# A hybrid decoder layer in split float32: who issues which transfer, and how many places the weights have

## The chip, the cores and the metric

The kernel runs on one core of a Trainium2 chip. The metric is device time of one execution in microseconds (us), as the median of three runs. The engines of the core are TensorE (PE, matmuls; PEld are its weight loads), VectorE (DVE), ScalarE (ACT), GpSimd (POOL) and SyncE (SP, here an issuer of DMA transfers and nothing else). Every engine works through its own list of instructions in order and waits at the first one whose inputs or places are not ready. DMA transfers are issued by such an instruction too, on SyncE, ScalarE or GpSimd.

## The reference

One layer for 2048 new prompt tokens and for 8 x 8 sample tokens with a past, width 1024. Norms stand around both halves, the mixer has four retention heads and four gated-delta heads of 128, and the MLP has 4096 channels:

```python
h = _rmsnorm(x, pre_mix_w)
m, S_r, S_g, new_conv = _hybrid_mixer(h, ...)   # w_in: 1024 -> 4104
x = x + _rmsnorm(m, post_mix_w)                 # w_out is inside the mixer
h = _rmsnorm(x, pre_mlp_w)
f = jnp.square(jax.nn.relu(jnp.einsum('bld,df->blf', h, w_up)))
f = jnp.einsum('blf,fd->bld', f, w_down)
x = x + _rmsnorm(f, post_mlp_w)
```

```python
# a gated-delta head, for each chunk of positions
A = jnp.where(strict, bi[..., :, None] * kk * dmat, 0.0)
sol = lax.linalg.triangular_solve(eye + A, rhs, left_side=True, lower=True, unit_diagonal=True)
v_new = u - jnp.einsum('bhcd,bhde->bhce', w, S)
```

Retention keeps a decayed state per head; the delta heads have a short convolution ahead of them and solve a unit lower triangular system in each chunk. Outputs are the new rows and all states.

## The kernel before

**Products.** All is float32. A matmul operand is split into a high part and the rest, hi and lo, and each product is three matmuls (hi by hi, hi by lo, lo by hi). The prompt is worked in four blocks of T = 512 tokens; the second block also carries the 64 sample tokens. A block runs: statistics of its rows (`stats`, L485), its normed and split transpose (`prep`, L505), the input projection with the heads (`proj`, L1192), the output projection (`out_proj`, L1225), the second norm (`norm2`, L1269), the MLP (`mlp`, L1385) and the last norm with the residual (`finish_half`, L1396). The projections of a block are merged with the MLP of the block before it, so TensorE takes a few matmuls of the one and then of the other.

**Weights** (`load_unit`, L342). A unit is mostly four pieces. The first block loads a raw piece (L359, tag `wraw`), ScalarE writes its hi part (L360), and VectorE or GpSimd its lo part (L361, two pieces of four each), both into a 512 KB place with the tag `wpc`; the pair is stored in DRAM (L363, `ws`). Later blocks load the pair back (L365). There are WB = 6 places `wpc` and RB = 5 places `wraw`. The places `wraw` also take the rows and transposed features that `stats` and `prep` load (L490, L523), the mixer rows that come back from DRAM (`load_mix`, L568), and in the last block the residual rows `x1d` (L1423); in the other blocks those go through the two places `raw`.

**The delta heads' inverse** (`gdn_head`, L785 to L845). VectorE inverts small diagonal blocks; the data are turned between partitions by 19 small transfers a head in three stages: L797, L798 and L804; L823, L824 and L826; L839. After each stage VectorE waits for them. TensorE later transposes the result `XX` (L271). There are 16 heads over the four blocks.

**The MLP's square** (`up`, L1312): ScalarE writes relu into `raw` and its square, rounded to the hi part, into `fhi`; GpSimd squares `raw` exactly in place (L1325); VectorE takes the difference into `flo`.

**What sets the order.** TensorE's order is the order in which the program writes its instructions (L267, L271). A planner (`Weave`, L122) decides it when the program is built: it merges the generators of heads, projections and MLP by due times, which come from a table of latencies (L100). The other engines are ordered by the framework's scheduler, which lays out a timeline of its own (L1519) and so may put any instruction of SyncE, ScalarE, VectorE or GpSimd earlier or later than it is written. In the kernel before nearly all transfers are issued by SyncE.

Of the kernel before, what the change touches and what calls it, by code (L numbers as in the profile page):

```python
# [202 lines left out]
def hybrid_kernel(ctx: ExitStack, tc: tile.TileContext, I, O, NB: int, SB: int):  # L203
    nc = tc.nc
    PS = bass.MemoryType.PSUM
    NTM = T + NS
    WB = 6
    RB = 5
    HP = 100
# [132 lines left out]
    def load_unit(name, idx, n, ncol):  # L342

        src = I[name]
        for i in idx:
            src = src[i]
        per = 2 if ncol <= NU else 1
        w = per * ncol
        first = (name, idx) not in stored
        if first:  # L350
            stored[name, idx] = [wst.tile([P, 2 * w], F32, tag=nm("ws"), name=nm("ws")) for q in range(n // per)]
        his, los = [], []
        for q in range(n // per):
            fit = lambda t: t.rearrange("p (a c) -> p a c", a=per)
            both = page([P, 4 * NU], "wpc", F32R, bufs=WB)
            hi, lo = fit(both[:, :w]), fit(both[:, w:2 * w])
            if first:
                r = fit(page([P, 2 * NU], "wraw", bufs=RB)[:, :w])
                nc.sync.dma_start(r, src[:, per * q:per * (q + 1), :])  # L359
                act(hi, r, AF.Copy)  # L360
                tt(lo, r, hi.bitcast(F32), ALU.subtract, eng=(V, G)[TUNE["pool"][q % 4]])  # L361
                if NB > 1:
                    nc.sync.dma_start(stored[name, idx][q], both[:, :2 * w].bitcast(F32))  # L363
            else:
                nc.sync.dma_start(both[:, :2 * w].bitcast(F32), stored[name, idx][q])  # L365
            his.append(hi)
            los.append(lo)
        return (lambda k: his[k // per][:, k % per, :]), (lambda k: los[k // per][:, k % per, :])
# [43 lines left out]
    class Block:  # L412
# [72 lines left out]
        def stats(self):  # L485
            samp = self.samp
            ssh, ssq = small([P, 2, 8], "ssh", bufs=1), small([P, 8], "ssq", bufs=1)
            for t, (c0, rows) in enumerate(self.tiles):
                for hf in range(2):
                    xv = page([P, 2 * NU], "wraw", bufs=RB)[:rows, :T]  # L490
                    nc.sync.dma_start(xv, self.x_rows(t)[:, hf * T:(hf + 1) * T])
                    act(xv, xv, AF.Square, accum_out=ssh[:rows, hf, t:t + 1])
                    yield self.lat["st"]
# [11 lines left out]
        def prep(self):  # L505
            b, samp, NT, rstd = self.b, self.samp, self.NT, self.rstd
            yield self.lat["rstd"]
            hhi, hlo = self.place()
            dg = page([P, 2 * NU], "wraw", bufs=RB)[:, :T]
            tt(v4(dg), bc4(ident), per4(rstd[:, :NC]), ALU.mult)  # L510
# [11 lines left out]
            for k in range(KT):  # L522
                xk = page([P, 2 * NU], "wraw", bufs=RB)[:, :T]  # L523
                nc.sync.dma_start(xk, I["xpT"][b, k])
                parts = [(xk, 0, T, rB[0])]
                if samp:
                    xq = small([P, NS], "xq")
                    nc.sync.dma_start(xq, I["xsT"][k])
                    parts.append((xq, T, NT, rB[1]))
# [31 lines left out]
        def load_mix(self):  # L561
            self.mix = self.place()
            for e in self.order:
                for part in range(2 if self.samp else 1):
                    yield self.key(("e", "s")[part] + str(e))
                    if (e, part) in self.away:
                        c0, n = ((0, T), (T, NS))[part]
                        st = page([P, 2 * NU], "wraw", bufs=RB)[:, :n]  # L568
                        nc.sync.dma_start(st, self.mixd[e, :, c0:c0 + n])
                        self.split_mix(e, st, c0, n)  # L570
                W.signal(self.key(f"m{e}"), self.lat["mem"])
# [150 lines left out]
        def gdn_head(self, h):  # L722
# [73 lines left out]
            for c in range(NC):  # L796
                nc.sync.dma_start(prod[NB16 * c:NB16 * (c + 1), :BB * BB], cm2[:, c, :])  # L797
            nc.sync.dma_start(m2, prod[:nb, :BB * BB].unsqueeze(1).to_broadcast([nb, P // nb, BB * BB]))  # L798
            xtf = XT.rearrange("p c d -> p (c d)")[:nb]
# [3 lines left out]
            for c in range(NC):  # L803
                nc.sync.dma_start(w32[NB16 * c:NB16 * (c + 1)].rearrange("b j i -> b (j i)"), cm[:, c, :])  # L804
            two = lambda ap: ap.rearrange("p (u x) -> p u x", u=2)[:, :, :HB * BB].rearrange("p u (c r) -> p u c r", c=HB)
# [16 lines left out]
            blocks = xf[:nb, :BB * BB]  # L822
            nc.sync.dma_start(x1, blocks.rearrange("p (g x) -> p g x", g=g))  # L823
            nc.sync.dma_start(x2, xf[1:nb:2, :BB * BB].unsqueeze(1).to_broadcast([nb // 2, 2 * g, BB * BB]))  # L824
            for c in range(NC):
                nc.sync.dma_start(xc[:, c, :], blocks[NB16 * c:NB16 * (c + 1)])  # L826
            x1, z, ro = (ap.rearrange("p (r i) -> p r i", r=g) for ap in (x1, z, ro))
# [10 lines left out]
            for c in range(NC):  # L838
                nc.sync.dma_start(cm[:, c, :], ro[g * NB16 * c:g * NB16 * (c + 1)].rearrange("p r i -> p (r i)"))  # L839
            blk = lambda ap: ap.rearrange("p (b i) -> p b i", b=NB16).unsqueeze(1).to_broadcast([P, NC, NB16, BB])  # L840
# [68 lines left out]
        def gdn_sample(self, h):  # L909
# [4 lines left out]
            Ss = page([P, NSEQ, P], "Ss")  # L914
            nc.sync.dma_start(Ss, I["state_gdn"][h])
            pk = mx()
# [155 lines left out]
        def proj_ret(self, h):  # L1072
            samp, b = self.samp, self.b
            get, vd, gt, vds = self.vg[h]
            rt = get(1).rearrange("p (a i) -> p a i", a=2)
            nc.sync.dma_start(rt, I["rope"][:, :, b * T:(b + 1) * T])
            wu = load_unit("w_ret", (h, 0), KT, UNIT)
            qk = get(2).rearrange("p (a i) -> p a i", a=2)
            qks = rts = None
            if samp:  # L1080
                qks, rts = small([P, 2, NS], "qks", bufs=1), small([P, 2, NS], "rts", bufs=1)
                nc.sync.dma_start(rts, I["rope"][:, :, NB * T:])
            for a in range(2):
# [53 lines left out]
        def ret_sample(self, h):  # L1137
# [4 lines left out]
            Ss = page([P, NSEQ, P], "Ss")  # L1142
            nc.sync.dma_start(Ss, I["state_ret"][h])
            pt = mx()
# [80 lines left out]
        def out_proj(self, then=None):  # L1225
# [5 lines left out]
            for n, src in enumerate(("post_mix_w", "pre_mlp_w")):  # L1231
                w = page([P, D_MODEL], "kq", bufs=2) if self.b else page([P, D_MODEL], atag[n])
                nc.sync.dma_start(w, I[src].to_broadcast([P, D_MODEL]))
                wB.append(w)
# [34 lines left out]
        def norm2(self, t, m, sq, wB):  # L1269
# [9 lines left out]
            for hf in range(2):  # L1279
                x = page([P, NTM], "raw", bufs=2)[:rows, :T]  # L1280
                nc.sync.dma_start(x, self.x_rows(t)[:, hf * T:(hf + 1) * T])
                mh = mr[:, hf * T:(hf + 1) * T]
# [29 lines left out]
        def up(self, f, wu, ft, mi, n0, n1):  # L1312
# [10 lines left out]
            for hi, lo, v in parts:  # L1323
                act(hi, v, AF.Square)
            tt(r[:, :w], r[:, :w], r[:, :w], ALU.mult, eng=G)  # L1325
            for hi, lo, v in parts:
# [69 lines left out]
        def finish_half(self, t, u):  # L1396
# [7 lines left out]
            if u == 0 and t == 0:  # L1404
                self.r3 = small([P, 5, 2], "r3", bufs=1)
                self.w3 = page([P, D_MODEL], "vz")
                nc.sync.dma_start(self.w3, I["post_mlp_w"].to_broadcast([P, D_MODEL]))
            r = self.r3[:, t]
# [13 lines left out]
            for cols in half:  # L1422
                x = (page([P, 2 * NU], "wraw", bufs=RB) if tail else page([P, NTM], "raw", bufs=2))[:rows, :T]  # L1423
                nc.sync.dma_start(x, self.x1d[c0:c0 + rows, cols])
                stt(av[:, cols], av[:, cols], r[:rows, 0:1], x, ALU.mult, ALU.add)
# [106 lines left out]
```

## Time and profile before

| What | Value |
|---|---|
| Median of three runs | 3095.73 us (3091.30 to 3099.69) |
| Profiled execution | 3096.51 us |
| Its span, first to last instruction | 3094.7 us |
| TensorE busy | 2864.7 us, 93% |
| VectorE, ScalarE, GpSimd busy | 1552.2, 793.0, 603.0 us |
| Mean granted TensorE clock | 0.978 |
| Transfers on the hardware queue q1 | 229008 packets, 559.07 MB, 53.6% of 16 engines |
| Transfers on the software queue q0 | 7760 packets, 26.56 MB, 2.2% |

The span is the time from the first to the last instruction of the profiled execution. An engine that is busy for a small share can still be waited for, so the table says where to look and not what to gain. The granted clock is a share of TensorE's full speed, 2.4 GHz. Busy times of GpSimd are rough. Weights and the split copies make most of the traffic: 612 loads `wpc<-ws` of 512 KB and 204 stores `ws<-wpc`, all issued by SyncE.

### The profile page before, as it was taken

Reading aid. Unit: us, or ns where it says so; the run is one execution under the profiler, and the core shown is the slowest. Engines: PE = TensorE matmul, PEld = TensorE weight load, DVE = VectorE, ACT = ScalarE, POOL = GpSimd, SP = SyncE. Lnnn points to the kernel's source line nnn. Section 1 sums busy time; section 2 is a strip of 40 time slices with the busy share of each in tenths; the row PEclk is TensorE's granted clock in tenths of the full one; section 3 lists DMA queues with packets and bytes.
Section 4 is the critical chain, followed back from the end, with each engine's and each line's share of the span. In section 5 each row is a group of like instructions: output and inputs, shape, how many; then the busy total and the mean of one; then the engine's idle time right before and its main releaser. Section 6 shows DMA issues by size and latency. Waiting matters only on the chain.

```text
span 3094.7 us, 43223 instructions
## 1 busy us (share of the span) xinstructions
PE 2864.7 (93%) x16072; PEld 2456.4 (79%) x16072; DVE 1552.2 (50%) x3386; ACT 793.0 (26%) x2199; POOL 603.0 (19%) x610
## 2 busy tenths in 40 slices
PE   7888889999999898999999999899999999899998
PEld 6677788878888687888887888777878787787776
DVE  6978667474756526552535252456353544331112
ACT  4343423233323323322212222221112221210111
POOL 4232113231233313111101111211110111120101
PEclk9999999999999999999999999999999999999999
DMA  8645655666565666645444444565554554665554
GB/s 296 224 161 170 219 206 197 206 210 209 166 217 208 215 220 241 235 144 174 145 157 149 154 158 157 184 218 176 178 172 165 167 186 158 225 233 190 186 186 168
DMA packets 238130, 590.49 MB, mean 191 GB/s; under 512 B 63072, under 2 KB 71648, under 8 KB 237920
## 3 DMA queue, kind: packets, MB, share of 16 engines
q1 hardware_dynamic: 229008, 559.07, 53.6%
q0 software_dynamic: 7760, 26.56, 2.2%
q8 instruction: 127, 2.08, 0.3%
q10 hardware_dynamic: 1152, 2.10, 0.2%
q14 instruction: 83, 0.68, 0.1%
HBM read 443.02 MB, written 137.79 MB: 188 GB/s over the span
## 4 chain that ended last, share of the span: by engine, by line
PE 65%; DMA 14%; DVE 13%; issue 2%; SPq 2%; ACT 2%; POOL 1%; DVEq 0%; POOLq 0%; ACTq 0%
PE mm L267 57%; DMA wpc<-ws 8%; PE mx L267 7%; PE mx L271 2%; DVE ym L255 1%; DVE XX L255 1%; DVE mt L255 1%; DVE raw L255 1%; ACT junk L249 1%; DVE wpc L255 1%; DMA wraw<-in_x_prompt 1%; DVE XX L252 1%; DMA raw<-in_x_prompt 1%; DMA ym<-xf 1%; DMA ym<-ym 1%
## 5 line engine op out<-in xcount | busy, mean ns | idle before, releaser
L267 PE MATMUL mm<-ahi,wpc 128*128 128x512 f32 (+2 forms) x3040 | 880.3, 364 | 38.1 <-DMA wpc<-ws 32.6
L267 PE MATMUL mm<-wpc,fhi 128*128 128x512 f32 x2048 | 665.5, 406 | 47.9 <-DMA wpc<-ws 31.9
L267 PEld LDWEIGHTS mm<-ahi,wpc 128*128 128x128 f32 x3040 | 547.8, 191 | 127.9 <-DMA wpc<-ws 39.6
L267 PE MATMUL mm<-alo,wpc 128*128 128x512 f32 (+2 forms) x1520 | 540.4, 355 | 1.4 <-DVE alo L255 1.4
L267 PEld LDWEIGHTS mm<-wpc,fhi 128*128 128x128 f32 x2048 | 381.2, 192 | 150.7 <-DMA wpc<-ws 45.2
L267 PE MATMUL mm<-bhi,wpc 128*128 128x512 f32 (+2 forms) x1536 | 428.0, 353 | 11.9 <-DMA wpc<-ws 9.4
L267 PE MATMUL mm<-wpc,flo 128*128 128x512 f32 x1024 | 410.3, 401 | 8.0 <-DVE flo L255 8.0
L267 PE MATMUL mm<-wpc,bhi 128*128 128x256 f32 (+1 forms) x1664 | 301.2, 286 | 23.5 <-DMA wpc<-ws 22.2
L267 PEld LDWEIGHTS mm<-alo,wpc 128*128 128x128 f32 x1520 | 290.6, 191 | 34.4 <-DVE alo L255 1.6
L249 ACT ACTIVATE raw<-mm 128x512 f32<-128x512 f32 (+2 forms) x226 | 114.8, 509 | 786.9 <-PE mm L267 741.1
L267 PEld LDWEIGHTS mm<-bhi,wpc 128*128 128x128 f32 x1536 | 274.6, 190 | 46.2 <-DMA wpc<-ws 11.6
L255 POOL TENSOR_TENSOR raw<-raw 128x512 f32<-128x512 f32 (+2 forms) x166 | 151.1, 911 | 821.3 <-ACT fhi L249 670.2
L255 DVE TENSOR_TENSOR a<-a,mm 128x512 f32<-128x512 f32 x224 | 152.3, 684 | 255.9 <-PE mm L267 255.6
L267 PEld LDWEIGHTS mm<-wpc,bhi 128*128 128x128 f32 x1664 | 253.2, 190 | 28.2 <-DMA wpc<-ws 25.9
L267 PE MATMUL mm<-blo,wpc 128*128 128x512 f32 (+2 forms) x768 | 265.3, 345 | 0.0
L255 DVE TENSOR_TENSOR flo<-raw,fhi 128x512 fp32r<-128x512 f32 (+1 forms) x166 | 103.1, 622 | 307.7 <-POOL raw L255 307.7
L267 PEld LDWEIGHTS mm<-wpc,flo 128*128 128x128 f32 x1024 | 196.2, 192 | 56.3 <-DVE flo L255 10.8
L267 PE MATMUL mm<-wpc,blo 128*128 128x256 f32 (+1 forms) x768 | 216.4, 282 | 0.2 <-DVE blo L255 0.2
L255 POOL TENSOR_TENSOR wpc<-wraw,wpc 128x512 fp32r<-128x512 f32 (+1 forms) x104 | 145.7, 1413 | 338.4 <-ACT wpc L249 280.8
L249 ACT ACTIVATE wpc<-wraw 128x512 fp32r<-128x512 f32 (+1 forms) x208 | 129.4, 629 | 233.0 <-PE mm L267 151.6
L267 PEld LDWEIGHTS mm<-blo,wpc 128*128 128x128 f32 x768 | 146.3, 191 | 14.5
L267 PEld LDWEIGHTS mm<-wpc,blo 128*128 128x128 f32 x768 | 146.3, 190 | 0.4 <-DVE blo L255 0.4
(486 smaller groups left out, 3611.7 us busy)
## 6 DMA issues: line engine op xcount, KB each, us to landing
wpc<-ws SPq DMA_DIRECT2D x612, 512.0 KB
ws<-wpc SPq DMA_DIRECT2D x204, 512.0 KB
wraw<-in_w_up SPq DMA_DIRECT2D x64, 256.0 KB
wraw<-in_w_down SPq DMA_DIRECT2D x64, 256.0 KB
raw<-in_x_prompt SPq DMA_DIRECT2D x32, 256.0 KB
wraw<-in_w_ret SPq DMA_DIRECT2D x28, 256.0 KB
wpc<-ws SPq DMA_DIRECT2D x12, 528.0 KB
mixd<-raw POOLq DMA_DIRECT2D x24, 256.0 KB, 4.7
```

The source lines that it names most:

```text
L249: return A.activation(out, in_, f, **kw)
L252: return V.scalar_tensor_tensor(out=out, in0=in0, scalar=scalar, in1=in1, op0=op0, op1=op1)
L255: return (eng or V).tensor_tensor(out=out, in0=a, in1=b, op=op)
L267: return tc.keep_in_program_order(nc.tensor.matmul(out, lhsT, rhs, start=start, stop=stop))
L271: return tc.keep_in_program_order(nc.tensor.transpose(out, in_, ident[:rows, :rows]))
```

## The change

The places `wpc` become eight, the places `wraw` three, and a new tag `xin` has two places for a 128 x 512 tile. SyncE keeps the raw weights (L359), the split weights (L365) and the last block's `x1d`. GpSimd now issues the stores of split weights, all small transfers of the inverse, the sample states, the rotary tables, the norm weights, the rows `x` of the second norm, the `x1d` of the other blocks, and the mixer rows, which go to `xin`. ScalarE issues the loads of `stats` and `prep`, into `xin` too. The exact square at L1325 goes to ScalarE. The scratch that the framework keeps for GpSimd's transfers is set to 8192 bytes at the end of the program. In counts: GpSimd issues 642 more transfers (208 stores, 304 of the inverse, 130 others), ScalarE 58, and 166 squares change engine. The lines keep their numbers.

```diff
@@ -207,2 +207,2 @@
-    WB = 6
-    RB = 5
+    WB = 8
+    RB = 3
@@ -363 +363 @@
-                    nc.sync.dma_start(stored[name, idx][q], both[:, :2 * w].bitcast(F32))
+                    nc.gpsimd.dma_start(stored[name, idx][q], both[:, :2 * w].bitcast(F32))
@@ -490,2 +490,2 @@
-                    xv = page([P, 2 * NU], "wraw", bufs=RB)[:rows, :T]
-                    nc.sync.dma_start(xv, self.x_rows(t)[:, hf * T:(hf + 1) * T])
+                    xv = page([P, T], "xin", bufs=2)[:rows]
+                    nc.scalar.dma_start(xv, self.x_rows(t)[:, hf * T:(hf + 1) * T])
@@ -509 +509 @@
-            dg = page([P, 2 * NU], "wraw", bufs=RB)[:, :T]
+            dg = page([P, T], "xin", bufs=2)
@@ -523,2 +523,2 @@
-                xk = page([P, 2 * NU], "wraw", bufs=RB)[:, :T]
-                nc.sync.dma_start(xk, I["xpT"][b, k])
+                xk = page([P, T], "xin", bufs=2)
+                nc.scalar.dma_start(xk, I["xpT"][b, k])
@@ -528 +528 @@
-                    nc.sync.dma_start(xq, I["xsT"][k])
+                    nc.scalar.dma_start(xq, I["xsT"][k])
@@ -568,2 +568,2 @@
-                        st = page([P, 2 * NU], "wraw", bufs=RB)[:, :n]
-                        nc.sync.dma_start(st, self.mixd[e, :, c0:c0 + n])
+                        st = page([P, T], "xin", bufs=2)[:, :n]
+                        nc.gpsimd.dma_start(st, self.mixd[e, :, c0:c0 + n])
@@ -797,2 +797,2 @@
-                nc.sync.dma_start(prod[NB16 * c:NB16 * (c + 1), :BB * BB], cm2[:, c, :])
-            nc.sync.dma_start(m2, prod[:nb, :BB * BB].unsqueeze(1).to_broadcast([nb, P // nb, BB * BB]))
+                nc.gpsimd.dma_start(prod[NB16 * c:NB16 * (c + 1), :BB * BB], cm2[:, c, :])
+            nc.gpsimd.dma_start(m2, prod[:nb, :BB * BB].unsqueeze(1).to_broadcast([nb, P // nb, BB * BB]))
@@ -804 +804 @@
-                nc.sync.dma_start(w32[NB16 * c:NB16 * (c + 1)].rearrange("b j i -> b (j i)"), cm[:, c, :])
+                nc.gpsimd.dma_start(w32[NB16 * c:NB16 * (c + 1)].rearrange("b j i -> b (j i)"), cm[:, c, :])
@@ -823,2 +823,2 @@
-            nc.sync.dma_start(x1, blocks.rearrange("p (g x) -> p g x", g=g))
-            nc.sync.dma_start(x2, xf[1:nb:2, :BB * BB].unsqueeze(1).to_broadcast([nb // 2, 2 * g, BB * BB]))
+            nc.gpsimd.dma_start(x1, blocks.rearrange("p (g x) -> p g x", g=g))
+            nc.gpsimd.dma_start(x2, xf[1:nb:2, :BB * BB].unsqueeze(1).to_broadcast([nb // 2, 2 * g, BB * BB]))
@@ -826 +826 @@
-                nc.sync.dma_start(xc[:, c, :], blocks[NB16 * c:NB16 * (c + 1)])
+                nc.gpsimd.dma_start(xc[:, c, :], blocks[NB16 * c:NB16 * (c + 1)])
@@ -839 +839 @@
-                nc.sync.dma_start(cm[:, c, :], ro[g * NB16 * c:g * NB16 * (c + 1)].rearrange("p r i -> p (r i)"))
+                nc.gpsimd.dma_start(cm[:, c, :], ro[g * NB16 * c:g * NB16 * (c + 1)].rearrange("p r i -> p (r i)"))
@@ -915 +915 @@
-            nc.sync.dma_start(Ss, I["state_gdn"][h])
+            nc.gpsimd.dma_start(Ss, I["state_gdn"][h])
@@ -1076 +1076 @@
-            nc.sync.dma_start(rt, I["rope"][:, :, b * T:(b + 1) * T])
+            nc.gpsimd.dma_start(rt, I["rope"][:, :, b * T:(b + 1) * T])
@@ -1082 +1082 @@
-                nc.sync.dma_start(rts, I["rope"][:, :, NB * T:])
+                nc.gpsimd.dma_start(rts, I["rope"][:, :, NB * T:])
@@ -1143 +1143 @@
-            nc.sync.dma_start(Ss, I["state_ret"][h])
+            nc.gpsimd.dma_start(Ss, I["state_ret"][h])
@@ -1233 +1233 @@
-                nc.sync.dma_start(w, I[src].to_broadcast([P, D_MODEL]))
+                nc.gpsimd.dma_start(w, I[src].to_broadcast([P, D_MODEL]))
@@ -1281 +1281 @@
-                nc.sync.dma_start(x, self.x_rows(t)[:, hf * T:(hf + 1) * T])
+                nc.gpsimd.dma_start(x, self.x_rows(t)[:, hf * T:(hf + 1) * T])
@@ -1325 +1325 @@
-            tt(r[:, :w], r[:, :w], r[:, :w], ALU.mult, eng=G)
+            act(r[:, :w], r[:, :w], AF.Square)
@@ -1407 +1407 @@
-                nc.sync.dma_start(self.w3, I["post_mlp_w"].to_broadcast([P, D_MODEL]))
+                nc.gpsimd.dma_start(self.w3, I["post_mlp_w"].to_broadcast([P, D_MODEL]))
@@ -1424 +1424 @@
-                nc.sync.dma_start(x, self.x1d[c0:c0 + rows, cols])
+                (nc.sync if tail else nc.gpsimd).dma_start(x, self.x1d[c0:c0 + rows, cols])
@@ -1528 +1528 @@
-    nc = bacc.Bacc("TRN2", target_bir_lowering=False, num_devices=1)
+    nc = bacc.Bacc("TRN2", target_bir_lowering=False, num_devices=1, dynamic_dma_scratch_size=8192)
```

TensorE's order stays as it was but for the names of three tiles. SyncE's list goes from 1375 rows to 859, GpSimd's from 602 to 886 and ScalarE's from 1760 to 1982.

**First place: SyncE at the end of the second block.** The names `wpc_...<-ws_...` are loads of split weights into their places, the first four of the last unit before the merged stage and then of the next; `raw_...<-x1d_...` are residual rows for the last norm. Before:

```order
L365 DMA wpc_3413_18880<-ws_973_4987 128x1024
L365 DMA wpc_3414_18882<-ws_975_4988 128x1024
L1424 DMA raw_3407_18854<-x1d_4_115 128x512
L1424 DMA raw_3408_18857<-x1d_4_115 128x512
L1424 DMA raw_3418_18901<-x1d_4_115 128x512
L1424 DMA raw_3419_18904<-x1d_4_115 128x512
L365 DMA wpc_3415_18884<-ws_977_4989 128x1024
L365 DMA wpc_3416_18886<-ws_979_4990 128x1024
L365 DMA wpc_3438_19051<-ws_1026_5272 128x1024
L365 DMA wpc_3439_19053<-ws_1028_5273 128x1024
L1424 DMA raw_3424_18937<-x1d_4_115 128x512
L1424 DMA raw_3425_18940<-x1d_4_115 128x512
```

and now:

```order
L365 DMA wpc_3413_18880<-ws_973_4987 128x1024
L365 DMA wpc_3414_18882<-ws_975_4988 128x1024
L365 DMA wpc_3415_18884<-ws_977_4989 128x1024
L365 DMA wpc_3416_18886<-ws_979_4990 128x1024
L365 DMA wpc_3438_19051<-ws_1026_5272 128x1024
L365 DMA wpc_3439_19053<-ws_1028_5273 128x1024
L365 DMA wpc_3440_19055<-ws_1030_5274 128x1024
L365 DMA wpc_3441_19057<-ws_1032_5275 128x1024
```

The residual rows are gone from between the loads of weights, and eight of those follow each other.

**Second place: between the second and the third stage of the inverse, last delta head of the second block.** `ym_...<-xf` (L826) ends the second stage and `ym_...<-ym` (L839) is the third; `ws_...<-wpc_...` are stores of split weights, `wraw_...<-in_w_up` loads of raw ones. On SyncE before:

```order
L826 DMA ym_2006_9928<-xf_82 128x1x16 x4
L363 DMA ws_2099_10340<-wpc_2106_10349 128x1024
L359 DMA wraw_2144_10490<-in_w_up 128x512
L363 DMA ws_2101_10341<-wpc_2108_10355 128x1024
L359 DMA wraw_2146_10496<-in_w_up 128x512
L363 DMA ws_2103_10342<-wpc_2110_10361 128x1024
L359 DMA wraw_2175_10620<-in_w_up 128x512
L363 DMA ws_2132_10473<-wpc_2139_10477 128x1024
L359 DMA wraw_2177_10626<-in_w_up 128x512
L363 DMA ws_2134_10474<-wpc_2141_10483 128x1024
L359 DMA wraw_2179_10632<-in_w_up 128x512
L839 DMA ym_2006_9928<-ym_2006_9928 128x1x16 x4
```

On GpSimd now, with its splits of weights (`TENSOR_TENSOR wpc`) and reloads of mixer rows (`xin_...<-mixd`) in the same list:

```order
L826 DMA ym_2006_9928<-xf_82 128x1x16 x2
L363 DMA ws_2101_10341<-wpc_2108_10355 128x1024
L363 DMA ws_2103_10342<-wpc_2110_10361 128x1024
L363 DMA ws_2097_10339<-wpc_2104_10343 128x1024
L363 DMA ws_2099_10340<-wpc_2106_10349 128x1024
L255 TENSOR_TENSOR wpc_2139_10477<-wraw_2140_10478,wpc_2139_10477 128x512
L569 DMA xin_2001_9901<-mixd_3_114 128x512
L255 TENSOR_TENSOR wpc_2141_10483<-wraw_2142_10484,wpc_2141_10483 128x512
L363 DMA ws_2136_10475<-wpc_2143_10489 128x1024
L363 DMA ws_2138_10476<-wpc_2145_10495 128x1024
L839 DMA ym_2006_9928<-ym_2006_9928 128x1x16 x4
```

The stores have moved to GpSimd with the inverse's transfers and stand between its stages there, now beside GpSimd's own splits; the raw loads stay on SyncE.

## Rows read from the trace of the kernel before

**Rows 1.** The page's busy times: us, share of span, instructions

```profile
PE 2864.7 (93%) x16072; PEld 2456.4 (79%) x16072; DVE 1552.2 (50%) x3386; ACT 793.0 (26%) x2199; POOL 603.0 (19%) x610
```

**Rows 2.** Waits of TensorE: whom for, us in total, times, longest us

```profile
PE mm L267 <- DMA wpc<-ws: 96.2, 89, 5.6
PE mx L271 <- DVE XX L255: 23.6, 5, 10.1
PE mm L267 <- DVE flo L255: 8.0, 5, 3.1
```

**Rows 3.** Timeline of SyncE, end of the second block: start us, us, engine, line, operation

```profile
2006.12 6.34 SPq L1424 DMA_DIRECT2D raw<-x1d  x4
2012.55 2.17 SPq L365 DMA_DIRECT2D wpc<-ws  x4
```

**Rows 4.** Timeline of TensorE, matmuls behind a late reload; idle before in brackets

```profile
395.23 0.38 PE L267 MATMUL mm<-bhi,wpc 128*128 128x256 f32 x1 [2.57 <-DMA wpc<-ws]
...
1929.70 0.50 PE L267 MATMUL mm<-wpc,bhi 128*128 128x256 f32 x2 [2.14 <-DMA wpc<-ws]
...
1943.08 0.50 PE L267 MATMUL mm<-wpc,bhi 128*128 128x256 f32 x2 [1.64 <-DMA wpc<-ws]
...
2019.37 0.58 PE L267 MATMUL mm<-ahi,wpc 128*128 128x256 f32 x1 [4.96 <-DMA wpc<-ws]
...
3029.66 0.73 PE L267 MATMUL mm<-wpc,fhi 128*128 128x512 f32 x2 [0.33 <-DMA wpc<-ws]
```

**Rows 5.** Windows of 10 us: each engine's busy us, PEclk, DMA share, GB/s

```profile
1970.00:1980.00 10.00, 5.56 (x13) 4.40 (x14) 3.04 (x7) 1.44 (x4) 1.64 (x3) 0.68 0.91 363
...
2000.00:2010.00 10.00, 10.00 (x45) 7.38 (x44) 7.29 (x14) 4.77 (x12) 4.96 (x6) 0.96 0.24 88
```

**Rows 6.** Windows of two stages, same columns

```profile
1120.00:1220.00 100.00, 86.57 (x572) 79.37 (x571) 38.44 (x79) 27.48 (x85) 19.65 (x24) 0.91 0.60 205
...
1960.00:2040.00 80.00, 65.27 (x336) 53.34 (x336) 43.34 (x81) 23.34 (x62) 27.73 (x33) 0.89 0.61 213
```

**Rows 7.** Groups of GpSimd and ScalarE: busy us, mean ns

```profile
L255 POOL TENSOR_TENSOR raw<-raw 128x512 f32<-128x512 f32 (+2 forms) x166 | 151.1, 911 | 821.3 <-ACT fhi L249 670.2
...
L255 POOL TENSOR_TENSOR wpc<-wraw,wpc 128x512 fp32r<-128x512 f32 (+1 forms) x104 | 145.7, 1413 | 338.4 <-ACT wpc L249 280.8
L249 ACT ACTIVATE fhi<-raw 128x512 fp32r<-128x512 f32 (+1 forms) x166 | 88.5, 533 | 4.8
```

**Rows 8.** Transfers of single lines: issue ns minimum, median, maximum; landing

```profile
L839 SPq DMA_DIRECT2D ym<-ym x56: 543/596/644, 144.8 to 2583.8; - x56
...
L549 POOL DMA_DIRECT2D mixd<-raw x24: 539/625/769, 76.6 to 2505.9; - x24
...
DMA to landing us min/median/max: 1.9/3.1/4.5
...
L1427 ACTq DMA_DIRECT2D out_y_p<-a x8: 338/339/382, 3080.0 to 3089.1; - x8
```

**Rows 9.** Timeline, third inverse stage in the third and second block

```profile
1383.67 2.52 SPq L839 DMA_DIRECT2D ym<-ym  x4
...
1387.56 0.69 DVE L255 TENSOR_TENSOR ym<-ym,cst 128x512 f32<-128x512 f32 x1 [3.44 <-DMA ym<-ym]
...
1398.82 0.60 PE L271 MATMUL mx<-cst,XX 128*128 128x128 f32 x4
...
1039.54 1.11 PE L271 MATMUL mx<-cst,XX 128*128 128x128 f32 x4 [7.62 <-DVE XX L255]
```

**Rows 10.** Waits of SyncE, longest first, same columns as rows 2

```profile
SPq L363 <- DVE wpc L255: 132.9, 37, 10.5
```

**Rows 11.** Timeline, preparation of the fourth block and TensorE's first use

```profile
2034.99 2.61 ACT L249 ACTIVATE bhi<-wraw 128x512 fp32r<-128x512 f32 x4
...
2046.27 1.29 DVE L255 TENSOR_TENSOR blo<-wraw,bhi 128x512 fp32r<-128x512 f32 x2
...
2056.17 0.39 PE L267 MATMUL mm<-bhi,wpc 128*128 128x512 f32 x1
```

## The prediction

> **What bounds the kernel now.** I read the page first. TensorE works in 2864.7 of 3094.7 us [rows 1] and its order is written in the program (only TensorE's instructions are pinned), so the time is TensorE's work plus its waits, some 230 us. The table of waits, cut to TensorE, shows whom it waits for: 96.2 us in 89 waits go to `wpc<-ws`, the reloads of split weights; next come 23.6 us for the delta heads' inverse (DVE XX) and 8.0 us for `flo` [rows 2]. So the weight stream is the one wait of size, and I looked at why it is late.
>
> There are two reasons. In the output projection all four pieces of a unit are in use until its last token tile, and six places hold one unit and a half; SyncE can ask for the next pieces only as TensorE lets go, and TensorE waits 2.14 us at 1929.70, and 1.64 us at 1943.08 [rows 4]. This is depth. At the end of the second block SyncE stood in front of loads of `raw`, whose place DVE still held: its four of these stretch over 6.34 us from 2006.12, the weights are issued behind them at 2012.55, and TensorE waits 4.96 us [rows 3, 4]. This is a queue held up. I sorted the waits over 0.3 us, counting gaps in which neither matmul nor weight load runs (89 us in 68): 39 of them, 38 us, follow loads with none but weight loads on SyncE for the 7 us before (such as the last of the 68, at 3029.66), and 29, 51 us, follow other transfers (such as the first of them, at 395.23) [rows 4]. The transfer itself is not the bound: just before the late issue the DMA engines were busy 0.24 of the time, and when the backlog ran they moved 363 GB/s [rows 5].
>
> **The change, term by term.** The profiled execution took 3096.51 us (span 3094.7 and 1.8 around it), 0.8 above the median of the runs, 3095.73. I sum against 3096.5.
>
> *Weight loads: -80 us.* A unit now has its own four places beside the four of the one in work. The output projection's units follow each other at 13.4 us (1929.70, 1943.08 [rows 4]); four pieces are 2 MB, so they need 157 GB/s, under half of the 363. They are issued one unit ahead, and after the order below nothing but weights stands on SyncE. I take five sixths of the 96.2, since units at the joints (raw weights still being split, a place freed late) can still be late. Bounds: 0 (if something else paces) and 96.
>
> *Clock: -15 us.* The granted clock falls from 2.4 to 1.2 GHz behind such waits: 0.91 in 1120 to 1220, 0.89 in 1960 to 2040 [rows 6]. That is 9.0 + 8.8 = 18 us in these two stages. TensorE is idle for 28 of their 180 us, where a low clock costs nothing, and part of the waits there are not for weights; other stages add a little, so 15. Bounds 0 and 18.
>
> *The exact square to ScalarE: -3 us.* 166 squares leave GpSimd (911 ns each) and go to ScalarE (533 ns, by the square that it already does) [rows 7]; `flo` comes about 0.4 us earlier. Of the 8.0 us of waits for `flo` I take 3; one of 3 us fell where DVE was busy with the inverse, which this does not mend. ScalarE gains 166 x 0.53 = 89 us and stands at 26% [rows 1]; TensorE's own long matmuls hide it. If that cover fails, ScalarE's evacuations and hi squares come one square late and the 8.0 us could double: +8.
>
> *Small transfers of the inverse to GpSimd: +26 us.* Each of 16 heads has 19 transfers in three stages, each ended by a wait of DVE. The issue is alike: 596 ns on SyncE, 625 on GpSimd [rows 8]. The landing may differ. On SyncE four issues from 1383.67 end at 1386.19 and DVE goes on at 1387.56, so the last landed about 2.0 us after its issue began; for GpSimd the nearest row is a 256 KB store, 1.9 to 4.5 us, median 3.1 [rows 8, 9]. So -0.1 to +2.5 us a stage; I take +1.1, 3.3 us a head. In the last two blocks the result is ready two steps of 0.69 us after 1387.56, and TensorE comes at 1398.82, 9.8 us of slack [rows 9]: hidden. In the first two blocks TensorE already waits for a head (7.62 us at 1039.54 [rows 9]), so there I count all: 8 x 3.3 = 26; ends -2 and +60.
>
> *GpSimd's own queue: +5 us.* It gets 642 more issues (208 stores of split weights, 304 of the inverse, 130 others) of 0.62 us, 398 us, and loses 166 squares, 151 us: from 603 to some 850 us, 27% of the span. On average there is room; but its order is strict. In the second block stores, splits and reloads of mixer rows stand between the stages of a head (second pair of orders). A store waits for DVE's split: on SyncE those waits were 132.9 us in 37 [rows 10], 3.6 each; they now hold whatever is behind them on GpSimd, so splits and the next stage. I take 5 and keep the case in which it decides as a rival.
>
> *Feature loads on two `xin` places, issued by ScalarE: +6 us.* 58 issues of 0.34 us [rows 8] are 20 us of ScalarE, hidden. But in the preparation of the next block each load waits for DVE to leave the place two before it, and ScalarE stands in front of it, with PSUM evacuations behind. Per place: the issue 0.34, a load of some 2.0 us as above, a multiply on DVE, a copy on ScalarE, a difference on DVE of 0.65 us each (2.61 by 4, 1.29 by 2 [rows 11]), 4.3 us, with hand-overs 5; two places take turns, so eight loads take 20 us against 12.6 now (2034.99 to 2047.56 [rows 11]). TensorE first uses the result at 2056.17, 8.6 us later. What is left is near nothing to 8 us at three block joints; 6 in all, ends 0 and 24. Raw weights keep three places in place of five; ScalarE's and GpSimd's splits run ahead into eight places, so I put nothing for it. The tail's reloads of `x1d` do not stand before a weight load: 0.
>
> Sum: 3096.5 - 80 - 15 - 3 + 26 + 5 + 6 = 3035.5; I forecast **3035 us**, own range 2990 to 3065.
>
> **A rule that speaks against it.** The trace shows idle DMA engines (0.24) while SyncE waits on DVE with weights behind it [rows 3, 5]. The Trainium skill (DMA: Bandwidth & Descriptors, section Issuing engines are not separate DMA queues) says that transfers run on the same 16 engines whoever issues them, and several issuers save only issue time. By that the moves off SyncE buy nothing and the places alone count, the second rival's time. Here it was a wait in the issuer's order, not a shared engine, that held the weights, so the trace does not bear the rule out for this case.
>
> **Rivals.**
> First: one half works. If transfers or another wait replace the depth part, only the held-up loads gain: 51 of 89 of the 80, so 46, the clock 9, square 3, given back 37: 3096.5 - 58 + 37 = 3075. For: at 1970 to 1980 the DMA engines are 0.91 busy [rows 5]. Against: whole stages run at 205 and 213 GB/s [rows 6]. 0.18.
>
> Second: the moves off SyncE buy nothing, the places alone do: 34 + 6 (clock) + 3 against 37: 3091, no change to be told. For: small transfers take SyncE no longer than GpSimd [rows 8]. Against: 6.34 us at 2006.12. 0.08.
>
> Third, slower: GpSimd's order becomes the bound in the first two blocks. If each of three stages of 8 heads stands behind one split (1.41 us), one store (0.62) and that store's wait (3.6) [rows 7, 8, 10], that is 16.9 us a head, 135 us: 3096.5 - 98 + 135 = 3133. It decides from 12.3 us a head. For: the order, and no slack at 1039.54. Against: GpSimd is idle four fifths of the time. 0.16.
> GpSimd's 24 stores of 256 KB took 539 to 769 ns beside a busy DVE [rows 8]. The Trainium skill (SBUF — State Buffer, section A bandwidth-pool intuition that's wrong) has such an issue go from about 620 to 3100 ns when DVE holds their shared port; by its figures 19 issues would add up to 47 us a head, as an estimate, to this rival. The trace speaks against it.
>
> **How the numbers follow.** Forecast 0.54; first rival 0.18; second 0.08; third 0.16; better than 2990 (nothing given back: 3096.5 - 96 - 18 = 2982) 0.04. A measurement of this kernel can tell some 0.3% from no change, 9 us. Faster: 0.54 + 0.18 + 0.04 = 0.76; same 0.08; slower 0.16. The range 2980 to 3100 takes in all but the third rival and the ends of the fast cases.
>
> **What would show it.** Right: TensorE's wait for `wpc<-ws` under 20 us and its clock over 0.95 in the two stages; the load at the end of the second block issued while TensorE is still a unit back. The price: waits for DVE XX and XX's reloads growing, in the first 1120 us alone, from 24 to about 50 us. The third rival: GpSimd waiting for DVE or ScalarE before L804, L823 and L839, and DVE waiting over 5 us for `ym` in each head. The joints: TensorE waiting for `bhi` or `blo`. It would be wrong if the waits for weights stay over 40 us, or if new waits pass 60.

## The result, and the profile after

The changed kernel took 3118.28 us (median of six runs, 3116.79 to 3127.31) against 3097.64 for the kernel before on the same chip: a ratio of 1.0071, 95% interval 1.0052 to 1.0091. It is slower by some 22 us; 3035 was forecast. The profiled execution was the longest of the six, span 3125.5 us, so prices below come from medians and the trace says only where they arise.

The page's busy times stand to [rows 1] as follows; GpSimd rose from 603.0 us:

```profile
PE 2862.2 (92%) x16072; PEld 2469.1 (79%) x16072; DVE 1563.3 (50%) x3386; ACT 882.4 (28%) x2365; POOL 814.6 (26%) x1086
```

The weight waits went, as forecast. The table of TensorE's waits (whom for: us, times, longest) begins with other names:

```profile
PE mx L271 <- DVE XX L255: 37.5, 7, 14.4
PE mm L267 <- ACT raw L249: 34.9, 8, 9.7
PE mx L271 <- ACT mx L249: 31.3, 5, 12.6
PE mx L271 <- DVE mt L255: 17.9, 12, 5.5
PE mx L267 <- DVE raw L259: 16.9, 2, 8.5
```

No wait for `wpc<-ws` is left of the 96.2 us [rows 2]. SyncE's timeline at the end of the second block has one row where loads of `raw` had stood between weights [rows 3]:

```profile
1967.45 89.21 SPq L365 DMA_DIRECT2D wpc<-ws  x28
```

Since TensorE's order did not change, its n-th matmul is the same one in both traces, and the time between two of them can be set side by side. The third column of times is the kernel with eight places and nothing moved, the first experiment below; its profiled execution, too, was the longest of its runs (3025.50 us, median 3011.56).

| Stretch of TensorE's list | before, us (idle) | changed, us (idle) | eight places alone, us (idle) |
|---|---|---|---|
| first two blocks, matmuls 0 to 6000 | 1127.1 (102.5) | 1200.4 (155.9) | 1139.8 (108.0) |
| output projection, 6000 to 6400 | 59.6 (7.7) | 46.8 (0.0) | 47.5 (0.0) |
| joint to the next stage, 6400 to 6800 | 83.2 (9.5) | 102.9 (27.7) | 91.4 (15.8) |
| merged stage, 6800 to 10400 | 637.0 (33.1) | 598.8 (5.6) | 603.3 (8.5) |
| output projection and joint, 10400 to 11200 | 159.0 (21.7) | 150.9 (18.0) | 139.6 (7.6) |
| merged stage, 11200 to 14400 | 626.7 (29.3) | 606.2 (14.4) | 603.0 (11.6) |
| joint, 14400 to 14800 | 83.6 (4.5) | 105.5 (21.5) | 90.5 (7.2) |
| tail | 300.9 (4.0) | 293.9 (0.0) | 293.9 (0.0) |

The gain is there in the output projections, the merged stages and the tail. The changed kernel gives back 73 us in the first two blocks: 53 of them are idle time, and the granted clock of this stretch fell from 0.97 to 0.94. It also gives back some 20 us at two joints and 11 against eight places alone at the third (the row with an output projection in it). Windows over about the same matmuls (columns as in [rows 6]) show the clock of the stages that had 0.91 and 0.89 before: the first rose, the second has other waits now.

```profile
1196.00:1283.00 87.00, 76.01 (x550) 70.60 (x548) 32.30 (x70) 23.33 (x70) 22.88 (x35) 0.97 0.61 215
1993.00:2076.00 83.00, 65.78 (x361) 54.46 (x361) 48.19 (x82) 24.64 (x66) 31.62 (x47) 0.90 0.69 236
```

Two places show what new waits look like. First the last head of the second block. On GpSimd, stores, splits and state products stand between the first stage (L797, ended at 1068.15) and the copy of its result (L798). The rows below take GpSimd, DVE and TensorE in one list (idle time in brackets); the last row is TensorE, which waits for that head in the end:

```profile
1065.77 2.39 POOL L797 DMA_DIRECT2D ym<-ym  x4
...
1069.30 0.61 POOL L363 DMA_DIRECT2D ws<-wpc  x1
...
1079.54 2.05 POOL L255 TENSOR_TENSOR wpc<-wraw,wpc 128x512 fp32r<-128x512 f32 x1
1080.49 0.67 DVE L819 TENSOR_REDUCE xf<-XX 32x64 f32<-32x512 f32 x1
1081.54 0.59 POOL L798 DMA_DIRECT2D ym<-ym  x1
...
1091.57 0.21 DVE L255 TENSOR_TENSOR XTs<-cst,mx 64x64 f32<-64x64 f32 x1 [4.47 <-PE mx L271]
...
1099.62 0.59 DVE L255 TENSOR_TENSOR ym<-ym 128x256 f32<-128x256 f32 x1
...
1116.44 1.11 PE L271 MATMUL mx<-cst,XX 128*128 128x128 f32 x4 [10.75 <-DVE XX L255]
```

The same head before, SyncE and DVE:

```profile
1000.38 2.57 SPq L797 DMA_DIRECT2D ym<-ym  x4
...
1007.87 0.62 SPq L798 DMA_DIRECT2D ym<-ym  x1
...
1015.86 0.67 DVE L819 TENSOR_REDUCE xf<-XX 32x64 f32<-32x512 f32 x1
...
1020.63 0.59 DVE L255 TENSOR_TENSOR ym<-ym 128x256 f32<-128x256 f32 x1
```

From the end of L797 to L798 it was 4.9 us before and is 13.4 now. But this delay did not reach VectorE: the late copy landed 2.6 us after its issue, at about 1084.1, the other transfer that the product at 1099.62 reads (L823) landed at about 1085.7, and the product began without a wait for a transfer. What grew is VectorE's own list between L819 and that product: 25 instructions with waits for TensorE and ScalarE among them, 18.4 us, where 7 instructions and 4.1 us had stood. Up to the end of this head (0 to 1041 us before, 0 to 1118 now) VectorE waited less for the inverse's transfers than before, 16.2 us in all against 21.7. The two largest rows before, then now:

```profile
DVE XX L255 <- DMA XX<-ym: 7.7, 3, 3.8
DVE ym L255 <- DMA ym<-ym: 6.1, 4, 3.9
```

```profile
DVE ym L255 <- DMA ym<-ym: 6.9, 3, 3.3
DVE XX L255 <- DMA XX<-ym: 4.3, 2, 3.4
```

Still, over the eight heads of the first two blocks the time from the last reduction ahead of L797 to the finished `XX` rose from about 42 us in the mean to about 48. The framework's scheduler orders VectorE's list anew with every move, and no run here moves the issuer and keeps that order. So how much of a head's 6 us is GpSimd's list and how much VectorE's new order is not shown.

Second, the joint after that (GpSimd, DVE and TensorE in one list):

```profile
2054.86 0.58 POOL L1429 DMA_DIRECT2D out_y_p<-a  x1 [5.11 <-DVE a L252]
2055.44 1.07 POOL L1424 DMA_DIRECT2D raw<-x1d  x2
...
2065.62 0.75 DVE L252 SCALAR_TENSOR_TENSOR a<-a,r,raw 128x512 f32<-128x512 f32 x1 [6.29 <-DMA raw<-x1d]
...
2066.84 0.80 PE L267 MATMUL mm<-ahi,wpc 128*128 128x512 f32 x1 [9.69 <-ACT raw L249]
```

The store of a finished row waits for DVE, the loads of the next residual rows stand behind it on GpSimd, DVE waits for these, and they hold both places `raw`, which ScalarE needs to empty TensorE's PSUM. The experiments below come back to how much of the loss this chain explains.

### The profile page after: what moved, and what is told of

Its sections match the earlier page's. It is cut to its first block, busy times and chain, and to the rows that moved or that the text cites. A ratio compares the mean times of both kernels' runs of the same rounds, so it can differ in the third digit from the quotient of the medians.

```text
span 3125.5 us, 43206 instructions
## 1 busy us (share of the span) xinstructions
PE 2862.2 (92%) x16072; PEld 2469.1 (79%) x16072; DVE 1563.3 (50%) x3386; ACT 882.4 (28%) x2365; POOL 814.6 (26%) x1086
## 4 chain that ended last, share of the span: by engine, by line
PE 57%; DVE 11%; DMA 9%; issue 7%; POOL 2%; ACT 2%; DVEq 0%; ACTq 0%; POOLq 0%
PE mm L267 49%; PE mx L267 6%; DMA xin<-in_x_prompt 2%; PE mx L271 1%; DVE XX L255 1%; DVE ym L255 1%; DMA raw<-x1d 1%; DMA xin<-in_xpT 1%; DVE wpc L255 1%; DMA XX<-ym 1%; DMA x1d<-mt 1%; DVE mt L255 1%; DMA ym<-ym 1%; DMA ym<-xf 1%; DMA wraw<-in_w_down 1%
## 5 line engine op out<-in xcount | busy, mean ns | idle before, releaser
L255 DVE TENSOR_TENSOR flo<-raw,fhi 128x512 fp32r<-128x512 f32 (+1 forms) x166 | 95.1, 573 | 294.1 <-ACT raw L249 293.8
L363 POOL DMA_DIRECT2D ws<-wpc x208 | 116.7, 564 | 106.1 <-DVE wpc L255 67.8
```

Of the source, the lines that this page charges most:

```text
L255: return (eng or V).tensor_tensor(out=out, in0=a, in1=b, op=op)
L363: nc.gpsimd.dma_start(stored[name, idx][q], both[:, :2 * w].bitcast(F32))
```

## The experiments

Costs below are differences of ratios to the kernel before, times 3097.6 us. The half-widths of the intervals are 0.15% to 0.4%, so a cost is good to some 10 us. The recorded expectations use plain differences of medians, which can differ from these by that much.

**Eight places alone.**

```diff
-    WB = 6
+    WB = 8
-    nc = bacc.Bacc("TRN2", target_bir_lowering=False, num_devices=1)
+    nc = bacc.Bacc("TRN2", target_bir_lowering=False, num_devices=1, dynamic_dma_scratch_size=8192)
```

> The kernel before with eight weight places in place of six and the scratch of 8192 bytes, nothing else moved. Theory 1 (GpSimd as issuer of the inverse and of the residual rows costs the time, the places are sound): 89 us of weight waits fall to some 40, because loads can still be held up behind other transfers on SyncE; about 3040 to 3055, and nothing lost in the first two blocks. Rival (crowding: eight places let SyncE queue 4 MB ahead, 11.5 us at 363 GB/s, and every small transfer lands behind it): the first two blocks lose tens of us here too, and the time is 3095 or more. Second rival of the prediction (the places alone do the gain): near 3055.

Measured 3011.56 us, ratio 0.9719 (0.9689 to 0.9749): 87 us faster than before, so the moves cost 109. The waits of TensorE begin

```profile
PE mx L271 <- DVE XX L255: 24.7, 4, 12.4
PE mm L267 <- ACT raw L249: 18.9, 6, 6.3
PE mx L271 <- DVE mt L255: 18.9, 12, 5.3
```

and of the waits for reloads 0.8 us are left, though SyncE still stands in front of residual rows with weights behind them at the same place:

```profile
1961.36 6.32 SPq L1424 DMA_DIRECT2D raw<-x1d  x4
1967.77 2.27 SPq L365 DMA_DIRECT2D wpc<-ws  x4
```

A unit ahead in its own places covers this queue held up for 6 us. Both theory 1's 40 us of remaining waits and the crowding rival were wrong, and so was the price of the second rival.

**The scratch alone** (the second edit above without the first).

> The kernel before with the scratch of 8192 bytes and nothing else. If the eight places made the gain of 86 us, nothing: 3090 to 3106. If the scratch has a part in it, below 3085.

3093.84 us, 0.9992 (0.9973 to 1.0011): no change. The places made the gain.

**The moves alone** (the change with `WB = 6`, `RB = 5`, the old scratch and no `xin`).

> The change without its places: six weight places and five raw ones as before, no xin, all else as in the changed kernel. The prediction held that 51 of the 89 us of weight waits come from other transfers ahead of the loads on SyncE, which the moves take away. If so, the moves give about 51 us and cost about the 107 that stand between eight places alone and the changed kernel: near 3155. If the moves mend no weight wait, 3185 to 3205; if a short GpSimd scratch made the moves costly, 3100.

3188.92 us, 1.0303 (1.0261 to 1.0344): 94 us slower, and TensorE still waits for weights:

```profile
PE mm L267 <- DMA wpc<-ws: 81.5, 85, 2.9
```

With nothing but weights on SyncE (but for first loads and the tail's rows), 81.5 of the 96.2 us stay. So the split into 51 us of queue and 38 of depth failed; it had sorted the waits by what had been issued shortly before them, and with six places nearly all of it is depth.

**One part put back into the changed kernel.** Each returns `nc.sync` at some lines: `inverse_back` at the seven of the inverse (the first is shown), `stores_back` at L363, `rows_back` at L1281 and L1424, `x1d_back` at L1424 alone.

```diff
-                nc.gpsimd.dma_start(prod[NB16 * c:NB16 * (c + 1), :BB * BB], cm2[:, c, :])
+                nc.sync.dma_start(prod[NB16 * c:NB16 * (c + 1), :BB * BB], cm2[:, c, :])
...
-                    nc.gpsimd.dma_start(stored[name, idx][q], both[:, :2 * w].bitcast(F32))
+                    nc.sync.dma_start(stored[name, idx][q], both[:, :2 * w].bitcast(F32))
...
-                nc.gpsimd.dma_start(x, self.x_rows(t)[:, hf * T:(hf + 1) * T])
+                nc.sync.dma_start(x, self.x_rows(t)[:, hf * T:(hf + 1) * T])
...
-                (nc.sync if tail else nc.gpsimd).dma_start(x, self.x1d[c0:c0 + rows, cols])
+                nc.sync.dma_start(x, self.x1d[c0:c0 + rows, cols])
```

> The changed kernel with the 19 small transfers of the inverse issued by SyncE again. Theory 1: the first two blocks, which lost 75 us against before, get back 40 to 70 of them, so 3050 to 3080; the joints between blocks keep their loss of 20 us each. Rival (the stores of split weights on GpSimd hold up its splits and so everything): less than 20 us come back, 3100 or more. Crowding: less than 20 us, as well.

> The changed kernel with the stores of split weights issued by SyncE again. Theory 1 with order (the inverse's transfers stand behind stores and splits in GpSimd's list): 20 to 40 us of the 75 come back in the first two blocks, 3080 to 3100, unless SyncE's waits for the lo parts hold up raw weights. Theory 1 with landing alone (a transfer issued by GpSimd simply ends later): under 10 us, 3110 to 3120.

> The changed kernel with the residual rows of the second norm and of the last norm issued by SyncE again (two lines). Theory: at the three joints between blocks, where the changed kernel lost about 20 us each (TensorE waits for ScalarE's evacuation into raw 9.7 us and for mx 4 to 13 us, and DVE stood 6.3 us for residual rows issued by GpSimd), most comes back: 30 to 45 us, 3075 to 3090, but a few us of weight waits return. Rival (the two xin places make the joints late): under 10 us, 3108 or more.

> The changed kernel with one line put back: SyncE issues the residual rows x1d of the last norm. With both lines back it took 3080.7 against 3118.3. If the x1d rows make the loss (they come after the weights of the next stage are asked for, and hold the places raw that TensorE's evacuations need): 3080 to 3092. If the rows of the second norm do: 3105 to 3118.

| Put back | us | ratio (95%) | gives |
|---|---|---|---|
| inverse | 3075.42 | 0.9899 (0.9860 to 0.9937) | 53 |
| stores | 3094.54 | 0.9992 (0.9974 to 1.0010) | 24 |
| both residual rows | 3080.65 | 0.9931 (0.9906 to 0.9956) | 43 |
| `x1d` rows only | 3103.90 | 1.0025 (1.0004 to 1.0047) | 14 |

All three parts give back what theory 1 said, so no single one is the cause. Of the two lines of rows neither guess fitted: `x1d` makes about a third, and by difference the second norm's rows about two thirds; these were not put back alone.

**One part added to eight places alone.** The same lines the other way; `p_features` takes `xin`, `RB = 3` and ScalarE's loads, with mixer rows still issued by SyncE, and where a name ends in `square` the changed L1325 is in:

```diff
-            tt(r[:, :w], r[:, :w], r[:, :w], ALU.mult, eng=G)
+            act(r[:, :w], r[:, :w], AF.Square)
```

> Eight places alone (3011.6 us) plus one part of the change: the inverse's 19 transfers a head issued by GpSimd, the stores still on SyncE. Putting them back on SyncE had given the changed kernel 43 us. Theory of landing (a transfer issued by GpSimd reaches its reader later, whatever stands around it): about the same 40 us come here, 3045 to 3055. Rival, order (they stand in GpSimd's list behind the stores of split weights and their waits): with the stores on SyncE 0 to 20 us come, 3012 to 3030.

> Eight places alone plus one part of the change: the stores of split weights issued by GpSimd. Putting them back had given the changed kernel 24 us. If they harm only because the inverse stands behind them in GpSimd's list, nothing is lost here and SyncE loses 245 us of waiting for lo parts: 3000 to 3015. If they harm by themselves (GpSimd waits for VectorE's lo part with its own splits and squares behind it): 3020 to 3035.

> Eight places alone plus one part of the change: features loaded by ScalarE into two places xin, three places for raw weights, mixer rows into xin but still issued by SyncE. The prediction's term: 6 us, so about 3018. In the changed kernel the first 200 us lost 16 us before any reload of split weights, and ScalarE issues no later load than SyncE did, so the rival is that two xin places and three raw ones cost 10 to 20 us in the first block: 3025 to 3035.

> Eight places alone plus one part of the change: the exact square on ScalarE. The prediction's term: 3 us less, so about 3008. Rival: ScalarE's evacuations come one square later and the waits for flo and raw grow by up to 8 us: 3020.

> Eight places, the inverse's transfers on GpSimd and the exact square on ScalarE. With the square still on GpSimd the inverse had cost 60 us (3071.6), and TensorE's waits for flo had grown from 6.7 to 38.9 us. Theory (two costs on one engine: the squares stand behind the transfers in GpSimd's list, and the heads end later): the flo part of some 32 us goes, the heads' part stays, 3035 to 3050. Rival (all of it is late heads): 3060 to 3075.

> Eight places, the stores of split weights on GpSimd and the exact square on ScalarE. With the square on GpSimd the stores had cost 32 us (3043.2), with TensorE's waits for flo grown from 6.7 to 33.0 us. Theory (the stores cost only through the squares behind them): 3011 to 3018. Rival (the stores hold up GpSimd's splits of weights, and ScalarE and the raw weights behind these): 3030 to 3040.

> Eight places, the exact square on ScalarE, and the residual rows of the second norm and of the last norm issued by GpSimd (two lines). Theory (in GpSimd's list these loads stand behind its own stores of x1d and of the output, which wait for VectorE, so VectorE waits for rows at each joint): 25 to 40 us more than 3011, 3036 to 3051, all of it at the three joints. Rival (they cost only beside the stores and the inverse): under 10 us, 3011 to 3021.

> Eight places, the square on ScalarE, the inverse's transfers and the stores on GpSimd. Apart they cost 31 and 24 us over 3011. If they only add up: 3063 to 3070. If they stand in each other's way in GpSimd's list, the prediction's third rival: 3080 or more. If the one hides under the other: 3045.

| Eight places and | us | ratio (95%) | over its base |
|---|---|---|---|
| square | 3011.24 | 0.9715 (0.9693 to 0.9736) | -1 |
| features | 3023.27 | 0.9754 (0.9732 to 0.9776) | 11 |
| inverse | 3071.62 | 0.9906 (0.9875 to 0.9936) | 58 |
| stores | 3043.22 | 0.9818 (0.9790 to 0.9846) | 31 |
| square, inverse | 3042.22 | 0.9828 (0.9804 to 0.9852) | 35 |
| square, stores | 3035.96 | 0.9809 (0.9782 to 0.9837) | 29 |
| square, residual rows | 3043.46 | 0.9815 (0.9797 to 0.9832) | 31 |
| square, inverse, stores | 3072.36 | 0.9923 (0.9898 to 0.9948) | 64 |

The base of the lower four is the square's row, that of the upper four the places alone. The 11 us of the features are within the error. With the square left on GpSimd, the inverse's issues delay it: TensorE's wait for `flo` in `p_inverse` and, in the second fence, in `p_inverse_square`:

```profile
PE mm L267 <- DVE flo L255: 39.0, 13, 5.1
```

```profile
PE mm L267 <- DVE flo L255: 3.7, 4, 1.1
```

So the square, worth nothing by itself, is what keeps the inverse's price at 35 us; two costs on one engine, as expected. Again VectorE does not wait longer for the inverse's transfers: up to the last head of the second block these waits are 15.6 us in `p_inverse_square` and 26.4 in `p_square`. For the stores that theory fell: `flo` went from 32.9 to 6.8 us there too, and the time hardly moved. What they cost sits in the first two blocks, where the heads take about 45.5 us in the mean against 41.5 in `p_square` though the inverse is on SyncE. Which wait lengthens them is not settled. Inverse and stores add up, 35 + 29 = 64, and within the error do not harm each other beyond that. The rows' 31 us lie at the three joints (12, 9 and 16 us by matmul number). In `p_rows_square` GpSimd and DVE repeat the chain seen above:

```profile
1986.60 0.59 POOL L1429 DMA_DIRECT2D out_y_p<-a  x1 [6.93 <-DVE a L252]
1987.18 1.06 POOL L1424 DMA_DIRECT2D raw<-x1d  x2
...
1995.86 0.75 DVE L252 SCALAR_TENSOR_TENSOR a<-a,r,raw 128x512 f32<-128x512 f32 x1 [3.61 <-DMA raw<-x1d]
```

VectorE's waits do not show that this chain by itself makes the 31 us. It waits for these rows in `p_square` too, where SyncE issues them; of the three rows below the first is from `p_square`, the others from `p_rows_square`:

```profile
DVE a L252 <- DMA raw<-x1d: 24.9, 10, 6.5
```

```profile
DVE a L252 <- DMA raw<-x1d: 22.6, 11, 4.1
DVE kv L252 <- DMA x1d<-kv: 9.4, 4, 5.8
```

All its waits for rows of both norms fell from 60.0 to 38.6 us. What grew are its waits for GpSimd's own stores of `x1d` to land before it writes over the same tile in the second norm: 6.5 us to 22.3. The places `raw` come into it too, as the last experiment shows. Which of these makes how much of the 31 us is not settled.

**A version that beats both.** Eight places alone, and the residual rows of both norms in the five `wraw` places in every block.

```diff
-                x = page([P, NTM], "raw", bufs=2)[:rows, :T]
+                x = page([P, 2 * NU], "wraw", bufs=RB)[:rows, :T]
-                x = (page([P, 2 * NU], "wraw", bufs=RB) if tail else page([P, NTM], "raw", bufs=2))[:rows, :T]
+                x = page([P, 2 * NU], "wraw", bufs=RB)[:rows, :T]
```

> Eight places alone, with the residual rows of both norms loaded into the five places for raw weights in every block, not into the two places raw. TensorE still waits there 18.9 us for ScalarE's evacuation into raw and 13.3 for mx. If the shared places make these waits: 15 to 30 us less than 3011.6, so 2982 to 2997. If VectorE's chain of norms does: 3005 to 3013.

2995.23 us, 0.9661 (0.9647 to 0.9675): 18 us better than eight places alone and 105 better than before. TensorE's waits for ScalarE's evacuation into `raw` and for `mx` fell from 18.9 and 13.3 us to 1.2 each and are gone from the head of the list:

```profile
PE mx L271 <- DVE XX L255: 24.2, 4, 13.4
PE mm L267 <- DVE a L255: 19.6, 11, 2.9
PE mx L271 <- DVE mt L255: 18.9, 12, 5.3
```

The two shared places were what held the joints in this kernel, and more of them helped where another issuer had harmed.

## Why the prediction was wrong

The parts close the sum within the error: -87 for the places, -1 square, 35 inverse, 29 stores, 31 residual rows, 11 features make +18; the changed kernel stands at +22. The few transfers left (states, tables, norm weights, mixer rows) were not measured apart. The forecast was -61, so it missed by 83: 31 in the residual rows, 24 in GpSimd's queue, 9 in the inverse, 8 in weights and clock, and less elsewhere. Its own sign of being wrong came: TensorE's waits for `XX`, `raw` and `mx` grew by 72 us together, where 60 was the mark.

- **Weight loads and clock, -95 forecast: right in size, wrong in cause.** Measured 87 with the clock. The places do it by themselves. The reading that 51 us were SyncE's queue failed: taking the other transfers away left 81.5 us of waits, and leaving them in left 0.8. For that part the size was luck.
- **Inverse, +26: near in size, the mechanism not seen.** 35 us, inside the stated ends. The forecast had each stage end later by a longer wait of VectorE. Landing did get longer by about what was forecast: from the first issue of the third stage to VectorE's next step, where VectorE waited for it, it took 3.8 to 4.4 us on SyncE (13 of 14 heads, one 7.0) and 3.4 to 8.2 on GpSimd (nine heads, median 5.5). But VectorE's waits for these transfers did not grow in the first two blocks, where the heads did; VectorE's list had other work and other waits there. In the last two blocks the inverse stayed hidden, as forecast.
- **GpSimd's own queue, +5: the first step that failed.** The stores alone cost 29. The average share was quoted, 27%, and the busy share came out at 26%; it says nothing of a list in strict order. There GpSimd stood idle before a store for VectorE's lo part 40 times, 67.8 us in all in the changed kernel. The cost is shown; by which wait it reaches the heads is open.
- **The transfers priced at nothing: the second.** Of the 130 other issues only the tail's reloads were looked at, and the residual rows of the other joints were counted as weight loads set free. They cost 31 us. They went into a list with GpSimd's own stores, which wait for the engine that wants the rows, and VectorE came to wait for those stores as well.
- **Features, +6:** 11, within the error. Three places for raw weights in place of five were put at nothing, and that reading failed in the trace, whatever it cost: ScalarE waits for raw weights, and VectorE's wait for ScalarE's hi parts rose from 28.6 us before to 56.5, and in `p_features` to 44.7. **Square, -3:** nothing alone, 23 us as cover for the inverse.
- **Rivals.** The second had the mechanism (moves buy nothing, the places pay) and a wrong price, 43 for what is 87. The third had the side, but not its size: some 6 us a head, not 16.9, and the joints did as much. Nor did its sign show: in the first two blocks VectorE's longest wait for the inverse's transfers was 3.4 us, not over 5 in each head.
- **The rule set aside.** Here 94 us of moves bought 15 us of weight waits. The Trainium skill (DMA: Bandwidth & Descriptors, section Issuing engines are not separate DMA queues) has several issuers save issue time only. That the moves bought so little fits it, and the forecast was wrong to put it aside on one wait of 6.34 us. The issue itself stayed short on GpSimd, as forecast, though it is longer than SyncE's median of 392 ns before: the stores took

```profile
L363 POOL DMA_DIRECT2D ws<-wpc x208: 531/547/776, 13.9 to 1261.5; - x104
```

## What to carry to other kernels

When a stream is late, give it depth first and measure that alone: here a unit ahead hid a queue held up for 6 us as well as the loads' own latency. A transfer moved to a compute engine takes a place in that engine's list; write down what it then stands behind, and whether that waits, directly or round a corner, for the reader of the transfer. Look at every issue that moves, not at the class that the change is about. Where a scheduler orders the lists, look at the reader's list as well: a late issue in a trace is no cost until its reader is seen to wait for it.

## What was not expected of the hardware

A small load's landing depends much on what else is under way. The 26 residual rows `x1d` at the joints, mostly 256 KB, landed 3.0 to 11.1 us after the issue on GpSimd (median 4.4), and in `rows_back`, issued by SyncE, 2.5 to 11.1 (median 3.5). In the two runs together, the eight that took over 9 us had two to four weight loads of 512 KB under way when they were issued; of the 30 under 4.5 us, 25 had none. The issuer made about 1 us of difference in the median, the traffic up to some 8.
